# The weights of 128 output columns as one tile of 1024 columns instead of two of 512

## The chip, the cores and the metric

The kernel runs on one core of a Trainium2 chip. The metric is the device time of one execution in microseconds (us). Before the change the median of three runs is 1457.76 us (1455.7 to 1457.97).

## What is computed

The reference is a streaming encoder of two layers on 512 new prompt frames and on 8 running streams with 16 frames each, width 1024, in float32. Each layer is

```python
hn = _rms_norm(x, p['norm1'])
proj = hn @ p['w_in']                       # 1024 -> 1536
# RG-LRU on 256 columns, S5 on 256, sliding-window attention on the rest
mix = jnp.concatenate([out_a, out_b, out_c], axis=-1) @ p['w_out']
x = x + mix
hm = _rms_norm(x, p['norm2'])
act = jnp.square(jax.nn.relu(hm @ p['w_up']))   # 1024 -> 4096
x = x + act @ p['w_down']                   # 4096 -> 1024
```

and a last norm follows. The large part of the arithmetic is the four weight products.

## The kernel before

The 640 tokens are held in two groups `g` of 320 (256 prompt frames and 64 frames of four streams each), with features on the 128 partitions. The engines: TensorE (PE) multiplies, ScalarE (ACT) and VectorE (DVE) and GpSimd (POOL) do the elementwise work, and all DMAs are issued from SyncE's queue (SP, line 229).

A *unit* is the weight block of 128 output columns: 1024 input rows, lying as 8 blocks `k` of 128 x 128, so 1024 columns of float32 on 128 partitions, 512 KB. Products run in a rounded format, fp32r. To keep the precision both factors are split into a high part (rounded) and a low part (the remainder). `wload` (lines 232 to 235) loads half a unit, 4 blocks, 128 x 512, 256 KB, into a `raw` tile. `wunit` (237 to 247) does, for each of the two halves, the rounding `wh = raw` on ACT (line 243) and the subtraction `wl = raw - wh` on DVE (line 244). `product` (249 to 256) then runs over the 8 blocks with three matmuls each: high x high (252), high x low of the activations (253), low x high (254), 24 in all, into one PSUM bank of three with the tag `mm`. The tags `raw`, `wh` and `wl` have four buffers each of 128 x 512. The first unit of all is loaded ahead by `first` (line 976), in turn with the first pieces of x, and handed on as `raws`.

There are 272 units: per layer 12 for the input projection of each group, 8 for the output projection of each group, and for each of four chunks of the MLP 8 up and 8 down (`mlp`). Chunks 0 and 3 run for one group at a time and load their weights twice; chunks 1 and 2 use each unit for both groups, one product after the other. So 208 units serve one product and 64 serve two, 336 products or 8064 matmuls.

After a product its bank is evacuated: in the up part `t = max(pt, 0) * r` on DVE (951), its square on ACT (952), the rounded copy on POOL (`gcopy`, 156), the remainder on DVE (954); in the down part and the output projection the addition to `xT` on DVE (934), followed where a norm comes next by a scaled rounded copy on ACT (268), its remainder on DVE (269), a square on ACT (281) and a sum on POOL (288). Between the projections run the mixers: RG-LRU (`lru`), S5 (`s5`) and attention (`attention`), with many small operations on all engines, and at the start and before the second layer the constants of S5 (`s5_small`, `s5_const`, lines 382 to 527).

The program is written in Tile: buffers of one tag are handed round, all semaphores are set by Tile, and the order on each queue is fixed at build time by a planner with a model of the times (`tile.TileContext(nc, schedule_with_timeline_sim=True)`). On the chip each queue runs strictly in that order. A load into `raw` has to wait until the subtraction that last read the buffer is done, a rounding into `wh` and a subtraction into `wl` until the last matmul that read the buffer is done.

Of the kernel before, what the change touches and what calls it, by code (L numbers as in the profile page):

```python
# [11 lines left out]
F32 = mybir.dt.float32  # L12
# [38 lines left out]
def _cols(a):  # L51
    """(..., 128 r) vectors as columns."""
    a = np.asarray(a)
    return a.reshape(-1, 128).T
# [5 lines left out]
def _layout(inputs):  # L60
    """The arrays in the order in which the chip reads them: moves of elements only."""
# [6 lines left out]
    def tiles(w):  # L68
        # (1024, 128 n) -> (n, 128 p, 8 k, 128)
        return w.reshape(8, 128, -1, 128).transpose(2, 1, 0, 3)  # L70
# [9 lines left out]
    # small vectors, one column each  # L80
# [13 lines left out]
    # S5 input and output matrices: halves (re, im) and (im, re) on the partitions  # L94
# [53 lines left out]
def encoder_kernel(ctx: ExitStack, tc: tile.TileContext, a, o):  # L148
# [35 lines left out]
    # ------------------------------------------------------------ constants  # L184
# [4 lines left out]
    # the table of the exponentials comes in before the first load has landed  # L189
# [41 lines left out]
    # ------------------------------------------------------------ weights  # L231
    def wload(src, n):
        raw = wp.tile([128, 4, 128], F32, tag="raw", name="raw", bufs=4)
        dma(raw, src[:, 4 * n:4 * n + 4])
        return raw

    def wunit(src, raws=None):
        out = []
        for n in range(2):
            raw = raws[n] if raws else wload(src, n)  # L240
            h = wp.tile([128, 4, 128], F32R, tag="wh", name="wh")
            l = wp.tile([128, 4, 128], F32R, tag="wl", name="wl", bufs=4)
            act(h, raw, AF.Copy)  # L243
            tt(l, raw, h.bitcast(F32), OP.subtract)  # L244
            out.append((h, l))
        return out

    def product(w, m):
        pt = bank("mm")[:, 0:NG]
        for k in range(8):  # L250
            h, l = w[k // 4]
            mm(pt, lhsT=h[:, k % 4], rhs=m[:, k, 0], start=k == 0, stop=False)  # L252
            mm(pt, lhsT=h[:, k % 4], rhs=m[:, k, 1], start=False, stop=False)  # L253
            mm(pt, lhsT=l[:, k % 4], rhs=m[:, k, 0], start=False, stop=k == 7)  # L254
        return pt

    # ------------------------------------------------------------ norms
    class Norm:
# [41 lines left out]
        def rsqrt(self):  # L300
            """8/3 / sqrt(mean + eps) with the tokens on the partitions (0-127, 128-255, 192-319)."""
# [5 lines left out]
            # a first guess from the exponent, one step of second order and one of third  # L307
# [23 lines left out]
    # ------------------------------------------------------------ small vectors  # L331
# [6 lines left out]
    # ------------------------------------------------------------ accurate exp on small tiles  # L338
    def exp_small(out, x, n):
        """out = exp(x) on [128, n], to about one unit in the last place."""  # L340
# [16 lines left out]
    # ------------------------------------------------------------ LRU constants  # L357
# [24 lines left out]
    # ------------------------------------------------------------ S5 constants  # L382
# [49 lines left out]
    def cmul(eng, out, jout, wr, wis, z, jz, tmp, conj=False):  # L432
        """out = w z (stacked halves), jout = its halves swapped; wis has the half's sign."""
# [9 lines left out]
    def s5_const(L):  # L443
# [10 lines left out]
        # input matrices: slot s of a pair of groups is abar^(3-s) Bbar  # L454
# [15 lines left out]
        # output matrices  # L470
# [9 lines left out]
        # causal products inside a block: those with the block's last output, then the rows moved up  # L480
# [9 lines left out]
        # rotation tables by doubling  # L490
# [37 lines left out]
    # ------------------------------------------------------------ per layer small tensors  # L528
# [12 lines left out]
    # ------------------------------------------------------------ input projection  # L541
    def gelu2(eng, out, x):
        """out = 2 gelu(x)"""
# [79 lines left out]
    def in_proj(L, P, g, norm, raws=None):  # L623
# [13 lines left out]
        for n, (kind, i) in enumerate(units):  # L637
            in_evac(L, P, g, q, kind, i, product(wunit(w_in[n], raws if n == 0 else None), norm.h))
        return q

    # ------------------------------------------------------------ RG-LRU
    def lru(L, P, g, q, mix, c):
# [10 lines left out]
        for ct in range(2):  # L653
# [4 lines left out]
            # the newest rows before the convolution  # L658
# [7 lines left out]
            # decay a = exp(-2 w) and 1 - a^2 = tanh(w) (1 + a)^2  # L666
# [7 lines left out]
        # injection of the running states into the column before each sample  # L674
# [18 lines left out]
    # ------------------------------------------------------------ S5  # L693
    def s5(L, P, g, q, mix, c):
        K = P["S5"]
        u = q.ub
        # zz takes the place of U
# [5 lines left out]
        # inputs by blocks: rows (group of the pair, t, channel)  # L703
# [41 lines left out]
        # outputs  # L745
# [18 lines left out]
        # states after the last block  # L764
# [22 lines left out]
    # ------------------------------------------------------------ attention  # L787
    def attention(L, P, g, q, mix, c):
        # the samples' scratch
        kcT, p = c.at(0, 2, 2, 144), [c.at(640 + 288 * n, 2, 144) for n in range(2)]  # L790
        vc, pt = c.at(1280, 2, 2, 128), [c.at(640 + 288 * n, 2, 128) for n in range(2)]
        # those of the second pair of samples start at partition 32
        half = [slice(32 * n, 32 * n + 16) for n in range(2)]
        vn, pn = ([c.at(o, 2, 128)[h] for h in half] for o in (1792, 2048))
        # the prompt's, in the same place: keys' windows of 192 columns with 64 zeros on each side
# [179 lines left out]

    def first(g):
        norms[g] = Norm(g, n1(0))
        raws = []
        for k in range(0, 8, 2):
            dma(xT[:, g, k:k + 2], a["x"][g, :, k:k + 2])  # L980
            if g == 0 and k < 4:
# [74 lines left out]
```

## Time and profile before

| | |
|---|---|
| median of three runs | 1457.76 us (1455.7 to 1457.97) |
| span of the profiled execution | 1454.2 us |
| PE busy | 1404.7 us, 97% |
| DVE busy | 924.5 us, 64% |
| ACT busy | 662.4 us, 46% |
| POOL busy | 377.0 us, 26% |
| mean granted TensorE clock | 0.979 of full speed |
| moved by DMA | 156.27 MB, 107 GB/s over the span |

Durations come from one profiled execution, whose span is 3.6 us shorter than the median. Matmuls are pipelined: each is listed with about 313 ns though one starts every 147 ns, so the busy time of PE says only whether something was running on it. "Idle before, releaser" is the time for which an engine stood still before an instruction, and what let it go on. A line of the code can stand for many places, since `product` and `wunit` are called for every unit.

### The profile page before, as it was taken

Reading aid. Unit: us, or ns where it says so; the run is one execution under the profiler, and the core shown is the slowest. Engines: PE = TensorE matmul, PEld = TensorE weight load, DVE = VectorE, ACT = ScalarE, POOL = GpSimd, SP = SyncE. Lnnn points to the kernel's source line nnn. Section 1 sums busy time; section 2 is a strip of 40 time slices with the busy share of each in tenths; the row PEclk is TensorE's granted clock in tenths of the full one; section 3 lists DMA queues with packets and bytes.
Section 4 is the critical chain, followed back from the end, with each engine's and each line's share of the span. In section 5 each row is a group of like instructions: output and inputs, shape, how many; then the busy total and the mean of one; then the engine's idle time right before and its main releaser. Section 6 shows DMA issues by size and latency. Waiting matters only on the chain.

```text
span 1454.2 us, 25829 instructions
## 1 busy us (share of the span) xinstructions
PE 1404.7 (97%) x9540; PEld 1336.3 (92%) x9540; DVE 924.5 (64%) x1858; ACT 662.4 (46%) x1387; POOL 377.0 (26%) x565
## 2 busy tenths in 40 slices
PE   7699999999999999999999999999999999999997
PEld 7688688899999999999987898789999999999997
DVE  8999889856544344357687768875664434434564
ACT  6566565545422122135674667453543312313543
POOL 3847269401010011072244225320110100100111
PEclk9999899999999999999998999899999999999998
DMA  6232122344422222234422342224443222223452
GB/s 244 86 109 81 50 95 97 105 150 140 152 80 78 76 80 73 73 107 157 140 91 73 120 137 92 68 95 145 149 146 106 73 73 73 80 78 104 153 174 94
DMA packets 91389, 156.27 MB, mean 107 GB/s; under 512 B 14336, under 2 KB 18304, under 8 KB 91264
## 3 DMA queue, kind: packets, MB, share of 16 engines
q1 hardware_dynamic: 91264, 154.63, 32.0%
q8 instruction: 75, 1.23, 0.4%
q14 instruction: 50, 0.41, 0.1%
HBM read 151.02 MB, written 3.37 MB: 106 GB/s over the span
## 4 chain that ended last, share of the span: by engine, by line
PE 80%; DVE 11%; POOL 4%; issue 3%; ACT 2%; DMA 1%; SPq 0%; DVEq 0%; POOLq 0%
PE mm L254 24%; PE mm L252 24%; PE mm L253 24%; DVE wl L244 2%; PE att L899 1%; PE att L878 1%; PE s L755 1%; PE s L753 1%; PE att L176 1%; PE s L176 1%; PE fin L326 0%; PE att L663 0%; PE s L721 0%; PE s L779 0%; DVE bigr L269 0%
## 5 line engine op out<-in xcount | busy, mean ns | idle before, releaser
L254 PE MATMUL mm<-bigr,wl 128*128 128x320 f32 x2688 | 840.9, 314 | 22.6 <-DVE wl L244 22.6
L252 PE MATMUL mm<-bigr,wh 128*128 128x320 f32 x2688 | 840.2, 313 | 1.7 <-ACT wh L243 1.1
L253 PE MATMUL mm<-bigr,wh 128*128 128x320 f32 x2688 | 839.1, 313 | 1.0 <-DVE bigr L269 1.0
L243 ACT ACTIVATE wh<-raw 128x512 fp32r<-128x512 f32 x544 | 340.7, 630 | 494.4 <-PE mm L253 469.9
L254 PEld LDWEIGHTS mm<-bigr,wl 128*128 128x128 f32 x2688 | 509.8, 190 | 34.7 <-DVE wl L244 27.4
L252 PEld LDWEIGHTS mm<-bigr,wh 128*128 128x128 f32 x2688 | 509.4, 190 | 7.9 <-issue 5.0
L253 PEld LDWEIGHTS mm<-bigr,wh 128*128 128x128 f32 x2688 | 509.5, 190 | 6.9 <-issue 3.9
L244 DVE TENSOR_TENSOR wl<-raw,wh 128x512 fp32r<-128x512 f32 x544 | 399.7, 736 | 179.6 <-ACT wh L243 158.9
L156 POOL TENSOR_SCALAR bigr<-t 128x320 fp32r<-128x320 f32 x128 | 63.0, 493 | 566.3 <-ACT t L952 566.3
L934 DVE TENSOR_TENSOR xT<-xT,mm 128x320 f32<-128x320 f32 x160 | 77.7, 486 | 127.5 <-PE mm L254 127.4
L952 ACT ACTIVATE t<-t 128x320 f32<-128x320 f32 x128 | 59.9, 470 | 137.9 <-DVE t L951 132.3
L954 DVE TENSOR_TENSOR bigr<-t,bigr 128x320 fp32r<-128x320 f32 x128 | 69.7, 546 | 69.6 <-POOL bigr L156 69.3
L951 DVE SCALAR_TENSOR_TENSOR t<-mm,r 128x320 f32<-128x320 f32 x124 | 60.6, 488 | 81.5 <-PE mm L254 81.4
L288 POOL TENSOR_TENSOR ss<-ss,sq 128x320 f32<-128x320 f32 x58 | 56.9, 981 | 195.7 <-ACT sq L281 185.6
L833 POOL TENSOR_SCALAR att<-att,st 128x192 f32<-128x192 f32 (+3 forms) x40 | 37.2, 931 | 79.5 <-DVE st L831 43.6
L824 ACT ACTIVATE att<-att,st 128x192 f32<-128x192 f32 (+3 forms) x80 | 30.7, 389 | 28.3 <-DVE st L822 22.1
L269 DVE SCALAR_TENSOR_TENSOR bigr<-xT,sm,bigr 128x320 fp32r<-128x320 f32 x64 | 39.7, 629 | 3.8 <-ACT bigr L268 3.6
L268 ACT ACTIVATE bigr<-xT,sm 128x320 fp32r<-128x320 f32 x64 | 34.4, 558 | 11.1 <-DVE xT L934 7.8
L281 ACT ACTIVATE sq<-xT 128x320 f32<-128x320 f32 x66 | 30.4, 460 | 9.9 <-DVE xT L934 3.7
L878 PE MATMUL att<-kT,q 64*64 64x192 f32 (+2 forms) x256 | 28.1, 329 | 2.5 <-ACT att L824 2.1
L605 POOL TENSOR_TENSOR sw<-sw,cs 128x320 f32<-128x320 f32 x20 | 19.4, 969 | 33.6 <-ACT sw L604 28.3
L176 PE MATMUL att<-ident,att 128*128 128x128 f32 (+1 forms) x144 | 24.6, 280 | 3.2 <-DVE att L833 1.0
(287 smaller groups left out, 1078.6 us busy)
## 6 DMA issues: line engine op xcount, KB each, us to landing
raw<-w_up SPq DMA_DIRECT2D x192, 256.0 KB, 2.6
raw<-w_down SPq DMA_DIRECT2D x192, 256.0 KB, 2.6
raw<-w_in SPq DMA_DIRECT2D x96, 256.0 KB, 2.6
raw<-w_out SPq DMA_DIRECT2D x64, 256.0 KB, 2.5
xT<-x SPq DMA_DIRECT2D x8, 320.0 KB, 5.7
yT<-xT SPq DMA_DIRECT2D x8, 320.0 KB, 2.5
cs<-rope SPq DMA_DIRECT2D x4, 320.0 KB, 4.4
gg<-gg SPq DMA_DIRECT2D x2, 512.0 KB, 5.1
```

The lines of the kernel that those rows point to most:

```text
L156: return G.tensor_scalar(out, in_, 1.0, 0.0, OP.mult, OP.add)
L176: PE.transpose(out, in_, ident[0:n, 0:n])
L243: act(h, raw, AF.Copy)
L244: tt(l, raw, h.bitcast(F32), OP.subtract)
L252: mm(pt, lhsT=h[:, k % 4], rhs=m[:, k, 0], start=k == 0, stop=False)
L253: mm(pt, lhsT=h[:, k % 4], rhs=m[:, k, 1], start=False, stop=False)
L254: mm(pt, lhsT=l[:, k % 4], rhs=m[:, k, 0], start=False, stop=k == 7)
L288: G.tensor_tensor(self.ss, self.ss, sq, OP.add)
L934: tt(xT[:, g, k], xT[:, g, k], pt, OP.add)
L951: V.scalar_tensor_tensor(t, pt, 0.0, norm.r, OP.max, OP.mult)
L952: act(t, t, AF.Square)
L954: tt(am[:, f, 1], t, am[:, f, 0].bitcast(F32), OP.subtract)
```

## The change

Each unit becomes one tile of 128 x 1024 for `raw`, `wh` and `wl`, with two buffers of each tag in place of four of half the size; the bytes are the same. A unit is loaded with one DMA of 512 KB, rounded by one instruction of ACT and split by one of DVE. Only the first unit of the program keeps two loads, two roundings and two subtractions (`parts=2`) on the two halves of its one tile, and both of its loads are now issued behind the first piece of x (rows k = 0 and 1) and ahead of the second. `product` takes its blocks from the one tile. Comments are also gone from the file, so that line numbers shift.

```diff
-    def wload(src, n):
-        raw = wp.tile([128, 4, 128], F32, tag="raw", name="raw", bufs=4)
-        dma(raw, src[:, 4 * n:4 * n + 4])
+    def wload(src, parts=1):
+        raw = wp.tile([128, 8, 128], F32, tag="raw", name="raw", bufs=2)
+        for n in range(parts):
+            ks = slice(8 // parts * n, 8 // parts * (n + 1))
+            dma(raw[:, ks], src[:, ks])
         return raw

-    def wunit(src, raws=None):
-        out = []
-        for n in range(2):
-            raw = raws[n] if raws else wload(src, n)
-            h = wp.tile([128, 4, 128], F32R, tag="wh", name="wh")
-            l = wp.tile([128, 4, 128], F32R, tag="wl", name="wl", bufs=4)
-            act(h, raw, AF.Copy)
-            tt(l, raw, h.bitcast(F32), OP.subtract)
-            out.append((h, l))
-        return out
+    def wunit(src, raw=None, parts=1):
+        raw = wload(src) if raw is None else raw
+        h = wp.tile([128, 8, 128], F32R, tag="wh", name="wh", bufs=2)
+        l = wp.tile([128, 8, 128], F32R, tag="wl", name="wl", bufs=2)
+        for n in range(parts):
+            ks = slice(8 // parts * n, 8 // parts * (n + 1))
+            act(h[:, ks], raw[:, ks], AF.Copy)
+            tt(l[:, ks], raw[:, ks], h[:, ks].bitcast(F32), OP.subtract)
+        return h, l

     def product(w, m):
         pt = bank("mm")[:, 0:NG]
+        h, l = w
         for k in range(8):
-            h, l = w[k // 4]
-            mm(pt, lhsT=h[:, k % 4], rhs=m[:, k, 0], start=k == 0, stop=False)
-            mm(pt, lhsT=h[:, k % 4], rhs=m[:, k, 1], start=False, stop=False)
-            mm(pt, lhsT=l[:, k % 4], rhs=m[:, k, 0], start=False, stop=k == 7)
+            mm(pt, lhsT=h[:, k], rhs=m[:, k, 0], start=k == 0, stop=False)
+            mm(pt, lhsT=h[:, k], rhs=m[:, k, 1], start=False, stop=False)
+            mm(pt, lhsT=l[:, k], rhs=m[:, k, 0], start=False, stop=k == 7)
         return pt
...
     def first(g):
         norms[g] = Norm(g, n1(0))
-        raws = []
+        raw = None
         for k in range(0, 8, 2):
             dma(xT[:, g, k:k + 2], a["x"][g, :, k:k + 2])
-            if g == 0 and k < 4:
-                raws.append(wload(a["w_in"][0, 0], k // 2))
+            if g == 0 and k == 0:
+                raw = wload(a["w_in"][0, 0], 2)
```

## Rows read from the trace of the kernel before

**Rows 1.** The page, part 1: busy time, share of the span, instructions.
```profile
PE 1404.7 (97%) x9540; PEld 1336.3 (92%) x9540; DVE 924.5 (64%) x1858; ACT 662.4 (46%) x1387; POOL 377.0 (26%) x565
```

**Rows 2.** Busy by stretch: bounds, length, engines' busy us (instructions), clock, DMA share, GB/s.
```profile
0.00:75.00 75.00, 55.12 (x333) 50.41 (x334) 69.39 (x196) 47.07 (x98) 44.56 (x67) 1.00 0.46 161
75.00:145.00 70.00, 65.90 (x467) 58.85 (x466) 68.64 (x173) 46.34 (x117) 41.05 (x61) 0.93 0.31 96
...
200.00:300.00 100.00, 95.02 (x647) 82.23 (x646) 87.51 (x169) 51.14 (x135) 66.15 (x84) 0.95 0.32 103
300.00:400.00 100.00, 100.00 (x687) 99.80 (x686) 60.45 (x109) 47.52 (x84) 9.29 (x14) 1.00 0.45 149
400.00:620.00 220.00, 220.00 (x1502) 220.00 (x1502) 90.29 (x159) 54.95 (x95) 14.67 (x32) 1.00 0.23 76
```

**Rows 3.** Waits of PE: total us, times, longest; whole span, then 0 to 300.
```profile
PE mm L254 <- DVE wl L244: 22.6, 16, 3.0
PE mm L254 <- DVE wl L244: 17.0, 13, 2.8
```

**Rows 4.** Timeline of ACT, 362 to 372: start us, us, instruction [idle before <-releaser].
```profile
363.94 0.63 ACT L243 ACTIVATE wh<-raw 128x512 fp32r<-128x512 f32 x1 [0.44 <-PE mm L253]
365.70 0.63 ACT L243 ACTIVATE wh<-raw 128x512 fp32r<-128x512 f32 x1 [1.13 <-PE mm L253]
366.43 0.47 ACT L952 ACTIVATE t<-t 128x320 f32<-128x320 f32 x1
```

**Rows 5.** Timeline of DVE, 362 to 372.
```profile
361.43 0.69 DVE L244 TENSOR_TENSOR wl<-raw,wh 128x512 fp32r<-128x512 f32 x1 [0.49 <-ACT wh L243]
362.04 0.48 DVE L954 TENSOR_TENSOR bigr<-t,bigr 128x320 fp32r<-128x320 f32 x1
...
364.07 0.49 DVE L954 TENSOR_TENSOR bigr<-t,bigr 128x320 fp32r<-128x320 f32 x1 [0.53 <-POOL bigr L156]
364.60 0.69 DVE L244 TENSOR_TENSOR wl<-raw,wh 128x512 fp32r<-128x512 f32 x1
```

**Rows 6.** Groups by form: shapes xcount | busy us, mean ns | idle before, releasers.
```profile
L156 POOL TENSOR_SCALAR bigr<-t 128x320 fp32r<-128x320 f32 x128 | 63.0, 493 | 566.3 <-ACT t L952 566.3
...
L727 ACT ACTIVATE bigf<-s 64x320 f32<-64x320 f32 x32 | 13.8, 432 | 0.4
L741 ACT ACTIVATE bigf<-bigf 64x640 f32<-64x640 f32 x16 | 11.8, 737 | 6.2 <-DVE bigf L739 6.0
```

**Rows 7.** Timelines of DVE and of POOL, 648 to 658.
```profile
649.99 2.92 DVE L244 TENSOR_TENSOR wl<-raw,wh 128x512 fp32r<-128x512 f32 x2
...
650.86 1.50 POOL L514 TENSOR_TENSOR tab<-tab 128x496 f32<-128x496 f32 x1
```

**Rows 8.** Line 244 alone by stretch: length, DVE busy us (instructions), clock, DMA.
```profile
0.00:75.00 75.00, 19.40 (x25) 1.00 0.46 161
75.00:145.00 70.00, 19.42 (x23) 0.93 0.31 96
...
200.00:300.00 100.00, 27.97 (x34) 0.95 0.32 103
...
620.00:665.00 45.00, 17.56 (x21) 1.00 0.38 117
```

**Rows 9.** Timelines of PE around three of its waits.
```profile
206.55 0.64 PE L254 MATMUL mm<-bigr,wl 128*128 128x320 f32 x1 [2.81 <-DVE wl L244]
...
657.54 0.41 PE L254 MATMUL mm<-bigr,wl 128*128 128x320 f32 x1 [2.24 <-DVE wl L244]
...
913.01 0.63 PE L254 MATMUL mm<-bigr,wl 128*128 128x320 f32 x1 [2.99 <-DVE wl L244]
```

**Rows 10.** The page, part 6: loads, KB each, median us from issue to landing.
```profile
raw<-w_up SPq DMA_DIRECT2D x192, 256.0 KB, 2.6
...
gg<-gg SPq DMA_DIRECT2D x2, 512.0 KB, 5.1
```

**Rows 11.** Waits of SP's queue: total us, times, longest.
```profile
SPq L229 <- DVE wl L244: 965.7, 464, 10.0
```

More of the change, by code (lines that the diff above doesn't have):

```diff
@@ L621, in encoder_kernel, with in_proj @@
     kvs = {}
-    def in_proj(L, P, g, norm, raws=None):
+    def in_proj(L, P, g, norm, raw=None):
         if g == 0:
@@ L637, in in_proj @@
         for n, (kind, i) in enumerate(units):
-            in_evac(L, P, g, q, kind, i, product(wunit(w_in[n], raws if n == 0 else None), norm.h))
+            in_evac(L, P, g, q, kind, i, product(wunit(w_in[n], *((raw, 2) if n == 0 and raw is not None else ())), norm.h))
         return q
@@ L977, in first @@
         norms[g] = Norm(g, n1(0))
-        raws = []
+        raw = None
         for k in range(0, 8, 2):
             dma(xT[:, g, k:k + 2], a["x"][g, :, k:k + 2])
-            if g == 0 and k < 4:
-                raws.append(wload(a["w_in"][0, 0], k // 2))
+            if g == 0 and k == 0:
+                raw = wload(a["w_in"][0, 0], 2)
         for k in range(8):
             norms[g].add(k)
-        return raws
+        return raw
     warm = bank("fin")
@@ L991, in encoder_kernel @@
     dma(sm[:, 0:80], a["sm"][:, 0:80])
-    raws = first(0)
-    q0 = in_proj(0, None, 0, norms[0], raws)
+    raw = first(0)
+    q0 = in_proj(0, None, 0, norms[0], raw)
     dma(sm[:, 80:], a["sm"][:, 80:])
```

## The prediction

> **What bounds the kernel now.** I read the profile from the whole to the place. The busy line first [rows 1]: the matmul engine PE works 1404.7 of 1454.2 us. An edit that only makes other engines cheaper can therefore win, at the very most, the 49.5 us in which PE has nothing running. The table by stretches shows where these lie [rows 2]. From 300 to 620 us PE is busy without a gap; there 1502 matmuls take 220 us, 0.1465 us each, so one unit (128 output columns against one group of tokens, 24 matmuls) takes 3.52 us. The 50 us are lost at the start and in the stretches in which the mixers run: PE has 55.1 of the first 75 us, and it is DVE that is full there (69.4 of 75, then 68.6 of 70). The waits of PE name the cause [rows 3]: 22.6 us in 16 waits for `wl`, the low part of the split weights, which DVE writes; 17.0 us of it in 13 waits before 300 us. So the weights' path (DMA, ACT rounds, DVE subtracts, PE multiplies) is hidden nearly everywhere and shows at a few places where DVE is late.
>
> **The margin in the weights' path, before and after.** This is the step on which the sum rests. In a steady stretch ACT starts a rounding every 1.76 us [rows 4], half a unit, each time released by the last matmul that read the `wh` buffer (the releaser in the row is L253). DVE's subtraction for the rounding at 363.94 starts at 364.60 and takes 0.69, so it ends at 365.29, 1.35 us after the release [rows 4, 5]. With four half buffers, what was released now is used three halves later, at 5.28 us; its low part is read first by the third matmul, 0.29 us after that. The margin is 5.57 - 1.35 = 4.2 us.
> After the change there are two buffers of a whole unit. A buffer is free when a whole unit is through, and what goes into it is used one unit later: 3.52 + 0.29 = 3.81 us. The work in between grows. ACT: two rows of 640 and 320 elements differ by 305 ns, 0.95 ns an element [rows 6], so 512 more elements make 0.63 into 1.12 us. DVE: 512 and 320 elements take 0.69 and 0.49 us [rows 5], 1.04 ns an element, so 0.69 becomes 1.22. With the 0.03 us between the two, 2.37 us. The margin is 3.81 - 2.37 = 1.4 us: positive, so the steady stretches keep 3.52 us a unit, but 2.8 us smaller than before. Units that serve both groups (64 of 272) take 7.04 us and have 5.0 us.
>
> **What the change removes.** 272 roundings, 272 subtractions and 271 loads. One subtraction of 1024 for two of 512 saves 2 x 0.69 - 1.22 = 0.16 us of duration, but the next instruction of DVE starts 0.61 us after a subtraction that is listed with 0.69 [rows 5], so at the least 2 x 0.61 - 1.14 = 0.08 us of the queue. Where POOL works beside it, more is saved: at 650 us two subtractions took 2.92 us while POOL's L514 alone held 1.50 [rows 7]; a single one waits once instead of twice. In the four stretches with a full DVE or a late `wl`, the mean is 776, 844, 823 and 836 ns [rows 8], up to 0.15 over the clean 0.69; with that the saving is at most 0.16 + 0.15 = 0.31. I take the middle, 0.18: these rows hold 103 halves, 51.5 units, so 9.3 us (ends 4 and 16). Everywhere else PE is full and a shorter DVE or ACT gives nothing. ACT's saving, 2 x 0.63 - 1.12 = 0.14 a unit, goes at nothing: ACT is at 47 of 75 us in the fullest stretch [rows 2], and PE waits for DVE, not for it.
> The row at 650 us can be held against a page: the Trainium skill, "SBUF - State Buffer", section "Who interferes with whom", says that a DVE instruction with two SBUF inputs and a GpSimd instruction that reads SBUF shut each other out for the whole instruction. The row agrees. By that rule the merged subtraction also keeps POOL out for longer at a stretch, so of the pair's saving a part would come back as later POOL work.
>
> **What it adds.** First, the lost margin. Where PE already waits for `wl`, the margin is used up, and each such place now starts its lateness 2.8 us sooner: PE has idled 2.8 us more when DVE has caught up. The 16 waits lie in five places: the start up to 91 us, 148, 206, 651 to 657 and 913 us (the last waits of three of them are in [rows 9]). The waits inside a place count once, since after the first the margin is zero and stays so until DVE catches up. 5 x 2.8 = 14.0 us. Second, places where DVE is late today by less than 4.2 us and hidden: no row shows a wait there, so between 0 and three more places, 0 to 8.4; I take one, 2.8, because the waits that can be seen cluster in the full stretches. Third, the start: `first` now issues both halves of the first raw tile ahead of x's rows 2 and 3 instead of one. That pushes this x transfer by one 256 KB load: at 149 GB/s with the DMA engines 0.45 busy [rows 2], 331 GB/s, so 0.8 us; the earlier second half may pay it back. 0 to 0.8, I take 0.4.
> **Costs that I set to nothing, and their cover.** The evacuations: in ACT's queue the rounding waits at the head for PE, and behind it stands the copy of the unit just finished (L952, L268), which POOL (L156) and DVE (L954, L269) wait for. It now starts up to 0.5 us later. Nobody needs it before the last k of the next stage, 21 matmuls or 3.08 us later; 0.49 (L951, taken as long as L954 [rows 5]), by then ACT is free only at 1.15, + 0.47 (L952 [rows 4]) + 0.49 (POOL [rows 6]) + 0.49 makes 2.6. Cover 0.5 us; if it goes, 12 stage ends x 0.5 = 6 us. The loads: two raw buffers, each free when its subtraction is done. Their loop is load + rounding + subtraction against two units, 7.04 us. 256 KB land 2.6 us after issue [rows 10]; 256 KB more at 331 GB/s makes 3.4. The 512 KB load that the kernel has, gg, took 5.1 [rows 10], in company of others; 3.4 is nearer to the raw rows, which have the same source layout. Loop: 3.4 + 1.12 + 1.22 + 0.15 for hand-overs = 5.9 us, cover 1.1. SP's queue waits for `wl` before nearly every load (464 waits, [rows 11]) and the cache loads and outputs stand behind that; half as many waits, each one unit long, change nothing that PE waits for. The clock: from 75 to 145 and from 200 to 300 us the granted clock is 0.93 and 0.95 [rows 2], in stretches with PE waits, so some of the time ran at the lower level. More idling could add to that: 0 to 5 us (0.07 of 70 us), not in the sum.
>
> **Sum.** 14.0 + 2.8 + 0.4 - 9.3 = +7.9 us. The span was 1454.2, 3.6 us below the median 1457.76 of the runs (1455.7 to 1457.97); the difference goes onto either: span 1462, time 1465.7. About 0.2%, 2.9 us, is what a measurement of this kernel can tell from no change.
>
> **Rivals.** (a) The savings win and the margin costs little: faster. Mechanism: in the full stretches DVE is the bound, not the loop through the buffers; then the shorter margin only moves the same idle time, and each unit gives 0.08 to 0.31 us. For it: DVE is at 92 to 98% in the first 145 us [rows 2], and POOL's hold on it at 650 us [rows 7]. Against it: the waits end at `wl`, which starts only after a release by PE. It decides when the five places cost less than 9.3 us in all, under 1.9 each. At full saving, -16 + 0.4 + 5 x 1 = -10; at the middle -9.3 + 5 x 1 = -4. Time about 1450. A page gives the same sign: the Trainium skill, "VectorE: DVE Perf Modes", section "The TRN2 errata", has a fixed cost per instruction and advises large tiles; by its formula the 1024 take 1.22 us, as the rows gave.
> (b) Both cancel within 2.9 us: 1458.
> (c) The loop of the loads binds: from a landing time of 7.04 - 2.5 = 4.55 us the two raw buffers are too few. At gg's 5.1 each pair of units loses 0.56 us; the single-group units of the output projection and the MLP are 160 by the code, so 80 x 0.56 = 45 us: 1503.
> (d) The planner sets the queues anew, from coarser pieces, and puts a subtraction behind long DVE work at several more places: the forecast's mechanism with ten places and the clock's 5 us: 28 + 0.4 + 5 - 9.3 = +24: 1482.
>
> **How the numbers follow.** Forecast 0.42 (1461 to 1474), (a) 0.28, (b) 0.15, (c) 0.06, (d) 0.09. Faster by over 0.2%: 0.28; within: 0.15; slower: 0.57. The range takes in (a) to 1449, (b), the forecast and (d): 1449 to 1487; (c) and the far end of (a) stay out, together under 2 in 10.
>
> **What would show it.** In the profile after: 272 roundings near 1.12 and 272 subtractions of 1.22 to 1.35 us; raw loads of 512 KB near 3.4 us; 146.5 ns a matmul unchanged in the two-group stretch; PE's waits for `wl` (or, since the high part is now also late, for `wh`) up from 22.6 us to about 35 to 40 in all, at the same five places. DVE's busy time must fall by 45 to 60 us without PE gaining. I am wrong if the waits shrink (then a), if evenly spaced waits of 0.2 to 0.6 us appear in the single-group stretches (then c, or the evacuation cover), or if the mixers' stretches change length for reasons that are no wait for weights.

## The result and the profile after

The changed kernel takes 1474.65 us where the kernel before took 1457.26 us beside it: 1.0114 times as long, 95% interval [1.0095, 1.0133], or +17.4 us by the medians and 16.6 by the ratio. (The median counts one disturbed execution that the ratio leaves out; without it, 1473.1.) The forecast was +7.9 us: the sign was right and the time lies within the range, but the loss is more than twice as large. The profile shown is of a second measurement of the same kernel, `e1_after_again` below, with a span of 1474.1 us, 19.9 longer than that of before.

The page of after, part 1, answers to [rows 1]: VectorE (DVE) works 33.7 us less, ScalarE 59.9 less, GpSimd (POOL) 68.8 more.

```profile
PE 1413.6 (96%) x9540; PEld 1340.7 (91%) x9540; DVE 890.8 (60%) x1587; ACT 602.5 (41%) x1116; POOL 445.8 (30%) x565
```

Groups by form (busy us, mean ns), then loads (KB, median us from issue to landing), against [rows 6] and [rows 10]:

```profile
L247 DVE TENSOR_TENSOR wl<-raw,wh 128x1024 fp32r<-128x1024 f32 x271 | 341.2, 1261 | 99.6 <-ACT wh L246 99.1
L246 ACT ACTIVATE wh<-raw 128x1024 fp32r<-128x1024 f32 x271 | 286.6, 1059 | 564.7 <-PE mm L255 486.9 <-DMA raw<-w_down 22.6 <-PE mm L256 18.0
L156 POOL TENSOR_SCALAR bigr<-t 128x320 fp32r<-128x320 f32 x128 | 110.9, 868 | 609.5 <-ACT t L954 604.5 <-ACT st L831 4.9
...
raw<-w_up SPq DMA_DIRECT2D x96, 512.0 KB, 3.4
```

The durations are those of the prediction: 1.06 us for a rounding (forecast 1.12), 1.26 for a subtraction (1.22 to 1.35), 3.4 us for a load (3.4). The waits of PE (total us, times, longest; after's lines 254 and 256 are 252 and 254 of before) answer to [rows 3]. The first two rows are the changed kernel's whole span, the next two the same from 0 to 305 us, and the last is the wait for `wh` of the kernel before:

```profile
PE mm L256 <- DVE wl L247: 29.0, 22, 4.3
PE mm L254 <- ACT wh L246: 5.3, 7, 2.1
...
PE mm L256 <- DVE wl L247: 17.8, 10, 4.3
...
PE mm L254 <- ACT wh L246: 2.5, 2, 2.1
...
PE mm L252 <- ACT wh L243: 1.1, 1, 1.1
```

34.3 us are waited for the two parts of the weights in 29 waits, 23.7 in 17 before (22.6 for `wl`, 1.1 for `wh`). Up to 300 us it is 20.3 against 18.1; most of the growth is behind that point.

To see where the time went, the span is cut at the same products in both kernels (a product is 24 matmuls; the cuts are the starts of products 0, 44, 72, 135, 207, 240, 304 and 335). Columns as in [rows 2]. First the kernel before:

```profile
0.00:299.75 299.75, 268.12 (x1777) 231.78 (x1777) 267.46 (x620) 178.00 (x428) 172.41 (x236) 0.95 0.33 109
299.75:400.85 101.10, 101.10 (x694) 100.90 (x693) 61.00 (x109) 47.73 (x84) 9.29 (x14) 1.00 0.45 150
400.85:622.53 221.68, 221.68 (x1514) 221.68 (x1513) 90.21 (x158) 54.95 (x95) 14.67 (x32) 1.00 0.23 77
622.53:983.83 361.30, 352.44 (x2419) 321.49 (x2418) 268.06 (x541) 211.86 (x483) 136.02 (x205) 0.97 0.33 108
983.83:1101.65 117.82, 117.82 (x806) 117.63 (x805) 71.21 (x126) 54.00 (x94) 10.22 (x16) 1.00 0.45 148
1101.65:1326.84 225.19, 225.19 (x1539) 225.19 (x1537) 91.42 (x160) 55.60 (x96) 14.68 (x32) 1.00 0.23 76
1326.84:1438.30 111.46, 111.46 (x764) 111.27 (x763) 68.96 (x125) 58.73 (x104) 18.05 (x28) 1.00 0.45 149
```

and the changed kernel:

```profile
0.00:309.41 309.41, 274.24 (x1801) 239.42 (x1802) 260.07 (x577) 172.16 (x387) 187.70 (x263) 0.92 0.32 105
309.41:416.39 106.98, 103.14 (x686) 101.63 (x685) 61.41 (x82) 40.23 (x54) 32.09 (x46) 0.98 0.44 138
416.39:638.07 221.68, 221.68 (x1515) 221.68 (x1514) 85.77 (x127) 47.19 (x64) 25.52 (x32) 1.00 0.24 77
638.07:997.96 359.89, 350.66 (x2403) 318.06 (x2402) 256.47 (x466) 197.16 (x409) 123.19 (x147) 0.98 0.34 109
997.96:1119.45 121.49, 119.84 (x807) 117.68 (x805) 69.69 (x93) 45.96 (x61) 15.52 (x16) 1.00 0.43 139
1119.45:1344.60 225.15, 225.15 (x1538) 225.15 (x1537) 86.29 (x128) 47.24 (x64) 25.50 (x32) 1.00 0.24 78
1344.60:1458.87 114.27, 112.73 (x764) 111.32 (x763) 64.91 (x95) 51.01 (x74) 34.65 (x28) 1.00 0.44 146
```

Rows 1 and 4 hold the mixers: +9.7 and -1.4 us. In row 1 PE stands still 3.5 us longer and is busy 6.1 us longer, at a granted clock of 0.92 instead of 0.95: 51.2 us of it at 1.2 GHz instead of 30.7, which is 10.2 us of lost cycles, as much as the whole row has grown. Rows 3 and 6 are the two-group chunks: not a tenth of a microsecond. Rows 2, 5 and 7 are the output projections and single-group chunks, in which PE had no gap before: +5.9, +3.7 and +2.8, together +12.4. The prediction set those three to nothing. What is left (the end) is -0.6.

**A change from up to down, in detail.** The last single-group chunk holds two of these places. The end of its first down product needs the last up unit's evacuation, so the planner runs the first two down products interleaved, in both kernels; their sums (L936 in after, L934 in before) come 1.02 us apart instead of 3.52. So two units give their buffers back together. Timelines (start us, us, instruction [idle before <-releaser]) in the changed kernel, of ACT, of DVE and of PE:

```profile
1378.90 1.06 ACT L246 ACTIVATE wh<-raw 128x1024 fp32r<-128x1024 f32 x1 [4.61 <-PE mm L255]
1379.87 0.45 ACT L276 ACTIVATE ss<-xT 128x320 f32<-128x320 f32 x1
1380.22 1.04 ACT L246 ACTIVATE wh<-raw 128x1024 fp32r<-128x1024 f32 x1
...
1379.00 0.49 DVE L936 TENSOR_TENSOR xT<-xT,mm 128x320 f32<-128x320 f32 x1 [2.97 <-PE mm L256]
1380.02 0.49 DVE L936 TENSOR_TENSOR xT<-xT,mm 128x320 f32<-128x320 f32 x1 [0.54 <-PE mm L256]
1380.43 2.35 DVE L247 TENSOR_TENSOR wl<-raw,wh 128x1024 fp32r<-128x1024 f32 x2
...
1379.68 0.31 PE L256 MATMUL mm<-bigr,wl 128*128 128x320 f32 x1
1380.01 0.42 PE L254 MATMUL mm<-bigr,wh 128*128 128x320 f32 x1
1380.27 0.30 PE L255 MATMUL mm<-bigr,wh 128*128 128x320 f32 x1
1381.32 0.42 PE L254 MATMUL mm<-bigr,wh 128*128 128x320 f32 x1 [0.75 <-ACT wh L246]
1381.57 0.31 PE L255 MATMUL mm<-bigr,wh 128*128 128x320 f32 x1
1381.72 0.39 PE L256 MATMUL mm<-bigr,wl 128*128 128x320 f32 x1
```

and of ACT and DVE at the same place of the kernel before:

```profile
1356.87 0.63 ACT L243 ACTIVATE wh<-raw 128x512 fp32r<-128x512 f32 x1 [0.61 <-PE mm L253]
1359.95 1.31 ACT L243 ACTIVATE wh<-raw 128x512 fp32r<-128x512 f32 x2 [2.45 <-PE mm L253]
...
1357.53 0.69 DVE L244 TENSOR_TENSOR wl<-raw,wh 128x512 fp32r<-128x512 f32 x1 [0.21 <-ACT wh L243]
1360.61 0.69 DVE L244 TENSOR_TENSOR wl<-raw,wh 128x512 fp32r<-128x512 f32 x1 [2.39 <-PE mm L253]
1361.22 0.48 DVE L934 TENSOR_TENSOR xT<-xT,mm 128x320 f32<-128x320 f32 x1
1361.62 0.68 DVE L244 TENSOR_TENSOR wl<-raw,wh 128x512 fp32r<-128x512 f32 x1
1362.24 0.49 DVE L934 TENSOR_TENSOR xT<-xT,mm 128x320 f32<-128x320 f32 x1
```

Before, the four half buffers come back spread out. The first half of the next unit is rounded at 1356.87 and subtracted at 1357.53, long before its product starts at 1362.05; only the second half waits for the interleaved pair, and its subtraction starts at 1360.61, 0.66 after its rounding. PE runs through at one matmul in 147 ns.

After, the next unit needs a whole buffer, which is free only when the first of the two products is through: its rounding starts at 1378.90. PE starts its last matmul of the pair at 1379.68 and is out of work at 1379.83, 0.9 us after the release, where the steady stretch leaves 3.52. With 0.29 us to the third matmul, which reads the low part, 1.2 us are there for rounding, hand-over and subtraction of 2.35 us; the second sum of DVE, which goes first, adds 0.4. PE waits while the rounding ends (1379.96), does two matmuls, and waits for the second rounding (it ends at 1381.26), which stood in ACT's queue behind the first and behind L276; the planner has put the next unit's first matmul here ahead of the third of this one. PE loses 0.2 + 1.2 = 1.4 us by the starts of its products. Worked out the same way, all six such changes lose 1.40 to 1.70, 8.7 in all; at each the refill starts 0.9 us before PE runs out. Four more changes of stage lose 0.73 each that they did not lose before: two from the output projection to up, and two, in the second mixers' stretch, from down to the next layer's input projection. Before, none of the six loses over 0.01.

**A place that moved.** In the first of the three stretches there is one more loss, 4.6 us at 327 us. POOL, DVE and PE in the changed kernel:

```profile
326.95 1.25 POOL L520 TENSOR_TENSOR tab<-tab 128x496 f32<-128x496 f32 x1
...
328.24 0.83 DVE L525 COPY tab<-s5s 128x1280 f32<-128x1280 f32 x1 [4.06 <-POOL tab L520]
328.98 1.22 DVE L247 TENSOR_TENSOR wl<-raw,wh 128x1024 fp32r<-128x1024 f32 x1
...
330.25 0.42 PE L256 MATMUL mm<-bigr,wl 128*128 128x320 f32 x1 [2.79 <-DVE wl L247]
```

DVE stands 4.06 us for POOL's constants of S5, with the subtraction behind it in its strict order. This is one of the five places of the prediction, the one at 651 to 657 us [rows 9], which cost 3.1 us (0.6 + 2.5 of two products) in before; the planner has put it elsewhere.

### The profile page after: what moved, and what is told of

Its sections match the earlier page's. It is cut to its first block, busy times and chain, and to the rows that moved or that the text cites. A ratio compares the mean times of both kernels' runs of the same rounds, so it can differ in the third digit from the quotient of the medians.

```text
span 1552.1 us, 24156 instructions
## 1 busy us (share of the span) xinstructions
PE 1502.1 (97%) x9540; PEld 1423.7 (92%) x9540; DVE 894.4 (58%) x1587; ACT 604.0 (39%) x1116; POOL 447.3 (29%) x565
## 4 chain that ended last, share of the span: by engine, by line
PE 82%; DVE 9%; POOL 4%; issue 3%; ACT 1%; DMA 1%; SPq 0%; DVEq 0%; POOLq 0%; ACTq 0%
PE mm L256 25%; PE mm L254 24%; PE mm L255 24%; DVE wl L247 2%; PE att L880 1%; PE att L901 1%; PE att L176 1%; PE s L757 1%; PE s L755 1%; PE s L781 1%; PE s L176 1%; PE att L665 1%; PE fin L328 0%; PE s L723 0%; DVE bigr L271 0%
## 5 line engine op out<-in xcount | busy, mean ns | idle before, releaser
L256 PE MATMUL mm<-bigr,wl 128*128 128x320 f32 x2688 | 880.5, 329 | 23.2 <-DVE wl L247 22.9
L254 PE MATMUL mm<-bigr,wh 128*128 128x320 f32 x2688 | 878.7, 327 | 6.4 <-ACT wh L246 5.3
L255 PE MATMUL mm<-bigr,wh 128*128 128x320 f32 x2688 | 876.4, 327 | 0.5 <-DVE bigr L271 0.4
L256 PEld LDWEIGHTS mm<-bigr,wl 128*128 128x128 f32 x2688 | 522.6, 195 | 37.4 <-DVE wl L247 29.2
L254 PEld LDWEIGHTS mm<-bigr,wh 128*128 128x128 f32 x2688 | 522.1, 194 | 17.4 <-ACT wh L246 8.8
L246 ACT ACTIVATE wh<-raw 128x1024 fp32r<-128x1024 f32 (+1 forms) x273 | 287.9, 1055 | 626.6 <-PE mm L255 591.4
L255 PEld LDWEIGHTS mm<-bigr,wh 128*128 128x128 f32 x2688 | 521.8, 194 | 6.4 <-issue 4.2
L247 DVE TENSOR_TENSOR wl<-raw,wh 128x1024 fp32r<-128x1024 f32 (+1 forms) x273 | 345.3, 1267 | 99.1 <-ACT wh L246 98.4
L156 POOL TENSOR_SCALAR bigr<-t 128x320 fp32r<-128x320 f32 x128 | 109.7, 859 | 660.9 <-ACT t L954 655.4
L936 DVE TENSOR_TENSOR xT<-xT,mm 128x320 f32<-128x320 f32 x160 | 77.8, 486 | 256.6 <-PE mm L256 256.4
L290 POOL TENSOR_TENSOR ss<-ss,sq 128x320 f32<-128x320 f32 x58 | 69.1, 1192 | 179.8 <-ACT sq L283 169.1
L271 DVE SCALAR_TENSOR_TENSOR bigr<-xT,sm,bigr 128x320 fp32r<-128x320 f32 x64 | 54.0, 855 | 3.6 <-ACT bigr L270 3.6
L607 POOL TENSOR_TENSOR sw<-sw,cs 128x320 f32<-128x320 f32 x20 | 24.5, 1223 | 39.1 <-ACT sw L606 33.7
L820 DVE TENSOR_REDUCE st<-att 128x2 f32<-128x384 f32 (+3 forms) x40 | 19.6, 490 | 21.0 <-PE att L880 20.7
```

The costliest lines, as they stand in the source:

```text
L156: return G.tensor_scalar(out, in_, 1.0, 0.0, OP.mult, OP.add)
L246: act(h[:, ks], raw[:, ks], AF.Copy)
L247: tt(l[:, ks], raw[:, ks], h[:, ks].bitcast(F32), OP.subtract)
L254: mm(pt, lhsT=h[:, k], rhs=m[:, k, 0], start=k == 0, stop=False)
L255: mm(pt, lhsT=h[:, k], rhs=m[:, k, 1], start=False, stop=False)
L256: mm(pt, lhsT=l[:, k], rhs=m[:, k, 0], start=False, stop=k == 7)
```

## The experiments

M is the forecast's theory (the smaller margin in the weights' path), P the planner's order, L the loads, D the long subtraction, A the long rounding. All ratios are against runs of the kernel before on the same chip. "Changes" is what PE loses at the six changes from up to down, worked out from the starts of the products.

### The changed kernel again

> The changed kernel once more, for a profile at the same clock as that of the kernel before. Theory M (the smaller margin between the release of a weight buffer and its use): 1474 us, the waits of the matmul engine for the low or high part of the weights 35 to 42 us in all against 23.7, the further 5 us in stretches at the lower clock. Theory P (the planner's new order of the queues moves the mixers' work, no wait for weights): the same time, but waits for weights below 30 us and the lost time in longer mixer stretches (75 to 290, 727 to 987 us in the kernel before). Theory L (the loads): roundings wait for loads, over 20 us in sum in the single-group stretches.

Measured: 1476.37 us, ratio 1.0121 [1.0092, 1.0149]. Its trace is the one above; changes 8.7 us. The waits of 34.3 us lie just under M's 35 to 42 and above P's bound of 30. The first mixers' stretch is longer, as P has it. Roundings wait 23 us for loads in the single-group stretches, which is L's sign; the next run shows what that is worth.

### Only the loads merged

```diff
-        h = wp.tile([128, 8, 128], F32R, tag="wh", name="wh", bufs=2)
-        l = wp.tile([128, 8, 128], F32R, tag="wl", name="wl", bufs=2)
...
+        for n in range(2):
+            ks = slice(4 * n, 4 * n + 4)
+            h = wp.tile([128, 4, 128], F32R, tag="wh", name="wh", bufs=4)
+            l = wp.tile([128, 4, 128], F32R, tag="wl", name="wl", bufs=4)
+            act(h, raw[:, ks], AF.Copy)
+            tt(l, raw[:, ks], h.bitcast(F32), OP.subtract)
```

> Only the load is merged (one raw tile of 1024 columns, two buffers); rounding and subtraction stay in halves with four buffers. Theory M: 1455 to 1461 us, since the margin at wh and wl is untouched. Theory L: 1468 to 1476 us. Theory P says nothing definite: any of 1450 to 1470 us, by what order the planner finds.

Measured: 1457.6 us, ratio 0.9994 [0.9973, 1.0014]; changes 0.05 us; the three single-group stretches as before, 330.4 us. Half as many loads, each landing in 3.4 us, cost and give nothing, though roundings wait 20 us for them in the single-group stretches here too. Rival (c) and theory L fall, and the loss is in rounding, subtraction and their buffers. PE's waits for weights add up to 13.2 us here, 23.7 in before, at the same time: their sum alone is no measure of the time.

### Whole tiles, in two steps of 512 columns

```diff
-        for n in range(parts):
-            ks = slice(8 // parts * n, 8 // parts * (n + 1))
+        for n in range(2):
+            ks = slice(4 * n, 4 * n + 4)
```

> As the changed kernel (whole tiles, two buffers, one load), but each unit is rounded and subtracted in two instructions of 512 columns into the halves of the tile. The first half is then ready 1.4 us after the release instead of 2.4 us, the margin 2.4 us instead of 1.4 (4.2 before). Theory M: about 10 us less than the changed kernel is slower than before, so 1463 to 1468 us. If the size of the instructions is what costs (a long subtraction in front of short work on DVE), 1458 us or less. If the release by whole units is all that counts, 1474 us.

Measured: 1460.87 us, ratio 1.0027 [1.0006, 1.0048]. That lies between M's 1463 to 1468 and the 1458 or less of the other theory. Changes 1.25 us instead of 8.7. So two whole buffers are not what costs most; it is the whole instruction on them.

### The kernel before with three half buffers of wh and wl

```diff
-            h = wp.tile([128, 4, 128], F32R, tag="wh", name="wh")
-            l = wp.tile([128, 4, 128], F32R, tag="wl", name="wl", bufs=4)
+            h = wp.tile([128, 4, 128], F32R, tag="wh", name="wh", bufs=3)
+            l = wp.tile([128, 4, 128], F32R, tag="wl", name="wl", bufs=3)
```

> The kernel before with three half buffers of wh and wl instead of four: the margin falls by one half, from 4.2 to 2.4 us, and nothing else changes. Theory M: at five places 1.8 us each, plus the hidden ones, 1466 to 1470 us, waits for the weights up to 32 us. Theory P (the margin is not what costs): within 5 us of 1457.

Measured: 1463.12 us, ratio 1.0039 [1.0022, 1.0056]. A smaller margin with no other edit costs 5.7 us by the ratio, less than M's 1466 to 1470 and about the bound of P; the waits for weights rise to 29.5 us, but the changes stay at 0.05 us.

### The high part whole, the low part in halves

```diff
-        l = wp.tile([128, 8, 128], F32R, tag="wl", name="wl", bufs=2)
+        l = [wp.tile([128, 4, 128], F32R, tag="wl", name="wl", bufs=4) for n in range(2)]
...
-            tt(l[:, ks], raw[:, ks], h[:, ks].bitcast(F32), OP.subtract)
+        for n in range(2):
+            ks = slice(4 * n, 4 * n + 4)
+            tt(l[n], raw[:, ks], h[:, ks].bitcast(F32), OP.subtract)
```

> As the changed kernel, but only the rounding is whole (one instruction of 1024 on ACT, two buffers of wh); the subtraction stays in halves with four half buffers. First low half ready 0.07 + 1.12 + 0.03 + 0.69 = 1.9 us after the release, margin 1.9 us (1.4 in the changed kernel, 2.4 in two steps, 4.2 before). Theory M, interpolated between the measured 2 us (margin 2.4) and 18 us (margin 1.4): 1464 to 1470 us. If the long subtraction on DVE is what costs (theory D): 1457 to 1461 us. If the long rounding on ACT is what costs (theory A): 1472 us or more.

Measured: 1468.67 us, ratio 1.0068 [1.0045, 1.0091]; changes 6.8 us. The two roundings at the same place, and the two waits of PE that follow:

```profile
1370.88 1.06 ACT L246 ACTIVATE wh<-raw 128x1024 fp32r<-128x1024 f32 x1 [4.75 <-PE mm L257]
1371.85 0.45 ACT L278 ACTIVATE ss<-xT 128x320 f32<-128x320 f32 x1
1372.21 1.04 ACT L246 ACTIVATE wh<-raw 128x1024 fp32r<-128x1024 f32 x1
...
1371.99 0.41 PE L256 MATMUL mm<-bigr,wh 128*128 128x320 f32 x1 [0.17 <-ACT wh L246]
...
1373.00 0.41 PE L258 MATMUL mm<-bigr,wl 128*128 128x320 f32 x1 [0.45 <-DVE wl L249]
```

With the whole rounding alone, 6.8 of the 8.7 us are there. The time lies in M's 1464 to 1470; D (1457 to 1461) and A (1472 or more) missed it.

### The high part in halves, the low part whole

```diff
-        h = wp.tile([128, 8, 128], F32R, tag="wh", name="wh", bufs=2)
+        h = [wp.tile([128, 4, 128], F32R, tag="wh", name="wh", bufs=4) for n in range(2)]
...
+        for n in range(2):
+            ks = slice(4 * n, 4 * n + 4)
+            act(h[n], raw[:, ks], AF.Copy)
+        for n in range(2):
+            ks = slice(4 * n, 4 * n + 4)
+            tt(l[:, ks], raw[:, ks], h[n].bitcast(F32), OP.subtract)
```

> The mirror: wh in halves with four half buffers as before, wl one whole tile with two buffers, written by two subtractions of 512. ACT is as before; the first low half can follow 0.7 us after the release of the whole wl tile, margin about 2.9 us. Theory M: 1457 to 1461 us. Theory A (long rounding): 1457 to 1460. If the release of wl by whole units is what costs: 1466 us or more.

Measured: 1459.49 us, ratio 1.0003 [0.9983, 1.0024]; changes 0.05 us. Two whole buffers of the low part, written in two steps, cost nothing that shows; M and A both had that.

### Whole tiles, in steps of 256 and 768 columns

```diff
-        for n in range(parts):
-            ks = slice(8 // parts * n, 8 // parts * (n + 1))
+        for ks in (slice(0, 2), slice(2, 8)):
```

> As the changed kernel, but each unit is rounded and subtracted in two steps of 256 and 768 columns. The first part is ready about 0.9 us after the release, margin 2.9 us; the second subtraction is 0.96 us long, ends about 2.3 us after the release and is needed at 4.7, margin 2.4. Theory M: 1457 to 1461 us, as the two equal steps. Theory D (the length of the subtraction in front of other work on DVE): between two steps (1461) and one (1475), about 1466.

Measured: 1474.16 us, ratio 1.0097 [1.0072, 1.0122], nearly as slow as the changed kernel, where M had 1457 to 1461 and D about 1466: both missed. Changes are only 0.4 us. The loss is another one. The second mixers' stretch (as row 4 above), first of the kernel with 512 and 512, then of this one:

```profile
634.29:985.46 351.17, 344.66 (x2398) 316.38 (x2397) 254.85 (x536) 201.57 (x479) 112.52 (x147) 0.99 0.35 112
...
634.56:1000.21 365.65, 358.94 (x2395) 327.13 (x2393) 260.83 (x536) 202.97 (x479) 112.09 (x147) 0.94 0.34 107
```

14.5 of the 15.8 us between the two spans lie here. PE is busy 14.3 us longer and stands still for about the same time (6.7 and 6.5 us): it works at a mean granted clock of 0.94 instead of 0.99, with 44.4 us at 1.2 GHz instead of 10.2, worth half of the 34.2, 17.1 us. The split of one instruction at another column thus moved the time by 10 us (by the ratios) to 13 (by the medians), over half of what the whole change did, and in the profile it did so in the mixers and at a lower clock.

### The changed kernel with x's order of before

```diff
...
-            if g == 0 and k == 0:
-                raw = wload(a["w_in"][0, 0], 2)
+            if g == 0 and k < 4:
+                raw = wload(a["w_in"][0, 0], slice(2 * k, 2 * k + 4), raw)
```

> The changed kernel with one thing undone: the second half of the first weights is issued behind the second piece of x, as before the change. By the prediction's term it is worth 0 to 0.8 us: 1473 to 1476. It also gives the planner a slightly other input; if what the change lost hung on one unlucky order of the queues (theory P), the time should move by 5 us or more in either direction.

Measured: 1478.2 us, ratio 1.0122 [1.0102, 1.0143]; changes 8.7 us. The order of the first loads is worth nothing that shows. The planner, given another start, came to nearly the same order from 180 us on (the place that moved, the six changes and the four others lose the same to 0.1 us), so the run tests the first loads and hardly another order.

### Two steps only at the changes of stage

```diff
-            w = wunit(a["w_up"][L, 8 * c + f])
+            w = wunit(a["w_up"][L, 8 * c + f], parts=2 if len(gs) == 1 and f < 2 else 1)
...
-            w = wunit(a["w_down"][L, c, k])
+            w = wunit(a["w_down"][L, c, k], parts=2 if len(gs) == 1 and k < 3 else 1)
```

> The changed kernel, with rounding and subtraction in two steps of 512 columns for 52 units only: f = 0 and 1 of the up part and k = 0, 1 and 2 of the down part in the chunks that run for one group (8 passes of such chunks and 5 units each are 40 uses; nothing else differs, and loads stay whole). M, as narrowed by the trace of the changed kernel: the single-group stretches lose their time at the changes from the output projection to up and from up to down, where two units give their buffers back together. Then the 1.2 to 1.4 us at each of the six changes up to down that showed it and the 0.7 us at three changes to up go to under 0.4 each: 6 x 1.0 + 3 x 0.5 = 7 to 9 us of the time beside the clock's loss, and 1464 to 1469 us where the changed kernel has 1474 to 1478. If the loss at these places is only one of many (the mixers' stretches pay most, or the clock does), the time stays within 3 us of the changed kernel, 1472 to 1479.

(The number of units is 40, not the 52 named first.) Measured: 1468.95 us, ratio 1.0085 [1.0066, 1.0104]: 7.4 us less than the changed kernel by the medians, 5.3 by the ratios. Changes 0.96 us. ACT and DVE at the place shown above:

```profile
1372.93 1.15 ACT L246 ACTIVATE wh<-raw 128x512 fp32r<-128x512 f32 x2 [4.36 <-PE mm L255]
...
1373.03 0.49 DVE L936 TENSOR_TENSOR xT<-xT,mm 128x320 f32<-128x320 f32 x1 [3.17 <-PE mm L256]
1373.60 1.29 DVE L247 TENSOR_TENSOR wl<-raw,wh 128x512 fp32r<-128x512 f32 x2
```

The first half's subtraction starts at 1373.60, 0.67 after the rounding and ahead of the second sum, as in before; PE loses 0.16 us. With 40 of 272 units in halves, the stretches of rows 5 and 7 are 118.4 and 112.0 us long, within 0.6 of before. So some 5 to 7 of the 17 us were lost at the changes of stage, and this run shows it by taking them away (the intervals of the two ratios just overlap, but the trace has the 7.7 us at the places where they were); the time lies at the upper end of what M expected (1464 to 1469). The kernel stays 12 us slower than before: the rest is elsewhere.

### The kernel before with subtractions of 256 columns

```diff
-            tt(l, raw, h.bitcast(F32), OP.subtract)
+            for ks in (slice(0, 2), slice(2, 4)):
+                tt(l[:, ks], raw[:, ks], h[:, ks].bitcast(F32), OP.subtract)
```

> The kernel before, with each of the 544 subtractions of 512 columns in two of 256: 0.69 us become 2 x 0.42 by the 1.04 ns an element, 0.15 us more a half, 0.30 a unit, and DVE is busy some 70 to 80 us longer in all; the last step ends 0.15 us later, so the margin of 4.2 us hardly shrinks. The prediction's saving (9.3 us for one instruction fewer in 51.5 units of the full stretches, 0.18 each) says with its sign turned: two more a unit, 2 x 0.18 x 51.5 = +18 us, by its low end 8: 1467 to 1477. If DVE's instruction count is worth nothing because the late units wait in the loop through the buffers and in the order of the queue, the time stays within 4 us of 1458.

Measured: 1472.1 us, ratio 1.0101 [1.0077, 1.0125], +14.7 us: within the 8 to 18 us that the savings' term says with its sign turned. The two mixers' stretches (as rows 1 and 4 above), from the slowest of the six executions, with a span 23.8 us longer than that of before:

```profile
0.00:316.92 316.92, 276.81 (x1777) 237.52 (x1778) 275.31 (x711) 178.43 (x428) 163.70 (x236) 0.90 0.33 104
...
639.71:1007.64 367.93, 358.77 (x2418) 327.82 (x2417) 279.48 (x684) 212.03 (x483) 129.77 (x205) 0.94 0.35 106
```

All of it is here (+17.2 and +6.6 us; every other stretch has the length of before to 0.1 us). DVE has 7.9 and 11.4 us more to do in them, so work of DVE in these stretches does reach the end. But the clock fell too, from 0.95 to 0.90 and from 0.97 to 0.94, and the waits for `wl` halved, to 11.4 us: PE now waits for the mixers' own operations. What the longer DVE work cost directly and what came through the clock, the run doesn't separate.

### All together

The margin is worked out for each kernel as in the prediction: from the release of a buffer to the first matmul that needs what goes into it, less the work in between, with 0.63 and 1.06 us for a rounding, 0.69 and 1.26 for a subtraction and 0.03 between (for 256 and 768 columns 0.42, 0.83 and 0.45, 0.99). Where a unit has several pieces, the smallest margin stands.

| kernel | margin, us | changes, us | three single-group stretches, us | ratio |
|---|---|---|---|---|
| before | 4.2 | 0.05 | 330.4 | 1 |
| loads merged | 4.2 | 0.05 | 330.4 | 0.9994 |
| low part whole, two steps | 3.1 | 0.05 | 333.9 | 1.0003 |
| whole, 512 + 512 | 2.5 | 1.25 | 342.0 | 1.0027 |
| before, three half buffers | 2.5 | 0.05 | 337.6 | 1.0039 |
| whole, 256 + 768 | 2.4 | 0.4 | 343.3 | 1.0097 |
| high part whole | 2.0 | 6.8 | 340.2 | 1.0068 |
| changed kernel | 1.5 | 8.7 | 342.7 | 1.0121 |

The loss at the changes goes by the 1.2 us that are there from the release to the third matmul, and not by the steady margin. Until the first low part is ready it takes 0.90 us with 256 + 768 (no loss at five of the six changes), 1.35 with 512 + 512 (0.15 at five of them), 1.78 with the high part whole (1.1 to 1.16) and 2.35 in the changed kernel (1.40 to 1.70); in the last two DVE's second sum goes first. So M stands, narrowed to these changes and with the shorter time there. The whole rounding gives 6.8 of the 8.7 us; a whole subtraction behind roundings in halves was not run, so D's own share is open. P is not needed for it: the same loss stands at six places, and it went with the length of the instructions. In the kernels between, the single-group stretches also hold pieces of the mixers and the place of the S5 constants, moved there by the planner, so that neither their length nor the ratio is the margin's alone.

## Why the prediction was right in direction and wrong in its steps

The direction came out, and the time lies in the range; two steps of the sum did not come out, and that the part outside the changes of stage is near the forecast is in good part luck. By profile and profile, +19.9 us fall into three. (The profile of before lay 2.1 us under its median, so that much of it is no loss.)

- **The five places, the hidden place and the start, less the savings: forecast 14.0 + 2.8 + 0.4 - 9.3 = +7.9, measured +9.7.** That is +9.7 - 1.4 in the mixers' stretches, less the 1.7 and 2 x 0.73 of the changes of stage that lie in them, and the 4.6 of the place that moved. The sum is near, its terms are not. At the five places PE waited 23.7 us for weights before and waits 25.1 after: 14.5 and 13.0 at the start, 0.9 and 2.6 at 148 (now 146), 2.8 and 4.7 at 206 (now 218 to 223), 2.6 and 2.8 at 651 to 657 (now 330), 3.0 and 2.0 at 913. That is +1.4 by PE's listed waits, where 5 x 2.8 = 14.0 was summed, and the second step that failed: a place did not lose the 2.8 us by which its margin shrank. The one hidden place came about as forecast, 3.0 us at 768. The savings were under-sized, not over-sized: the subtractions of the first 300 us took 76.8 us for 91 halves, 1.69 a unit, and take 63.1 for 45 units, 1.40. So 0.29 a unit is saved where 0.18 was taken, and yet nothing is gained. What lengthened the first mixers' stretch goes in the profile with 10.2 us of cycles lost to the lower clock, which the sum left out; whether the clock is the cause of the length, no run separates.
- **The changes of stage: forecast 0, measured 8.7 + 4 x 0.73 = +11.6.** This is the step that failed: "The margin is 3.81 - 2.37 = 1.4 us: positive, so the steady stretches keep 3.52 us a unit". The margin was right (1.5 by the measured durations) and the steady stretches do keep 3.52. But the 3.81 us hold where a unit is released one unit, 3.52 us, ahead of its use. At a change from up to down the first two products end together, the first buffer comes back 0.9 us before PE needs what goes into it, and the margin is 1.2 - 2.35 = -1.1 us, with another 0.4 for the sum that goes first on DVE. The prediction did look at "12 stage ends", and only for the evacuation of the last product; it set these to nothing, and did not look at the release of the buffers there.
- **The rest, -1.4 us:** the end is 0.6 us shorter, and two products behind the first change to up PE waits 0.8 us less.

**The clock** was left out of the sum at 0 to 5 us. Its time at 1.2 GHz rises in the profile from 60.9 to 78.4 us, 8.8 us of lost cycles; but the profile of before has about the least such loss of all runs of before. Over the runs, span times what is missing of the clock is 35.0 us before (50 runs, 30.5 to 45.3) and 37.3 and 40.5 in the two measurements of after, so 2 to 6 us of the 17. The bound about held for this change by its runs, though not in the profile shown. It would not have held for its neighbours: 47.3 with subtractions of 256 columns, 50.1 with steps of 256 and 768. In the first 310 us of after there is a stretch in which PE shows no gap and DVE has room, and the clock is 0.73: from 225 to 250 us.

```profile
225.00:250.00 25.00, 25.00 (x144) 20.90 (x143) 16.50 (x30) 6.99 (x17) 18.06 (x28) 0.73 0.19 64
```

What lowers it is open: PE stands still 53.5 us in the kernel with 256 and 768, less than in the changed one (60.5), and has the lower clock. That the lost savings (0.29 a unit) went into it is argued and not shown.

**The rivals.** (a) falls by the result, though its mechanism is there: with DVE's work raised instead of lowered the time follows by 14.7 us. (b) falls by the result; (c) by the landing time of 3.4 us, under its limit of 4.55, and by the merged loads alone. (d), more places and a clock term, is the nearest in kind: there are ten more places at changes of stage. But it had them as an accident of the planner's order, and they come from the way in which the kernel changes stage (the same loss at each of the six changes from up to down).

**What would show it:** instructions, durations and the two-group stretch came as forecast; the waits came to 34.3 (35 to 40 forecast), but what they grew by is not at the same five places; DVE fell by 33.7 (45 to 60 forecast).

## What to carry to other kernels

Work out the margin of a rotating buffer for the moment when several buffers come back at once (a change of stage, an interleaved pair of products), not for the steady state: here 0.9 us were left instead of 3.52. Count the full length of every instruction in the refill queue. If a tile is merged for cheaper transfers, merge the load and leave the operations that refill what the bound engine reads in pieces: here the merged load alone cost nothing (0.9994), the merged instructions with it 1.2%. Compare kernels by stretches cut at the same work, since one that is slower in total can be so for reasons, such as the clock in a far stretch, that have nothing to do with the edit.

## What was not expected of the hardware

- **GpSimd's copy took longer where a unit's subtractions are one or stand together.** L156 (128x320) takes 493 ns on average in before [rows 6] and 868 in after; 497 with only the loads merged, 611 with whole tiles in two steps of 512, 724 with the low part alone whole, also in steps of 512. So the length of a subtraction is not all of it. POOL's busy time rose by 68.8 us, 47.9 of it in this line. The Trainium skill, "SBUF — State Buffer", "Who interferes with whom", has a DVE instruction with two SBUF inputs and a GpSimd instruction that reads SBUF shut each other out for the whole instruction; the trace agrees with it in direction. In the two-group stretches it cost nothing: 221.68 us in both kernels.
- **The granted clock differs between kernels with the same arithmetic.** The mean loss over a kernel's runs, span times what is missing of the clock, lies between 32.7 us (before with three half buffers) and 50.1 us (256 and 768).
